# Pinning TensorE to the order of the text in the mixer half of a hybrid encoder layer

## Chip, cores and metric

The kernel runs on one core of one Trainium2 chip. The metric is the device time of one execution in microseconds. TensorE does the matrix products and transposes, VectorE (DVE), ScalarE (ACT) and GpSimd (POOL) the elementwise work, SyncE (SP) issues nearly all transfers. TensorE writes to PSUM, eight banks here, which the other engines read and free.

## The reference, cut to what is computed

One layer on `x` of 1024 positions by 1024 channels in float32:

```python
u = rms_norm(x, g) @ w_in            # 3328 columns, split over three mixers
y_sb = stick_breaking_attention(q, k, v)   # 4 heads of 64, q and k normalised per head
#   z = q.k / 8;  w[t,s] = sigmoid(z[t,s]) * prod_{s<j<t} sigmoid(-z[t,j]),  s < t
y_ret = silu(r_g) * rms_norm(multiscale_retention(rotary(r_q), rotary(r_k), r_v))  # 8 heads
y_conv = silu(layer_norm(depthwise_conv31(glu(c_a, c_gate))))   # 256 channels
x = x + concat(y_sb, y_ret, y_conv) @ w_out
x = x + relu(rms_norm(x) @ w1)**2 @ w2     # 4096 hidden
```

## The kernel before

Products are computed at float32 accuracy from pairs: each operand is split into a high part and a remainder, and `mm3` (L117 to 120) issues three matmuls into one PSUM bank. A weight tile comes in by DMA, is rounded on ScalarE (L181), and its remainder is subtracted on GpSimd or VectorE (L182).

The mixer half, up to some 500 us of the trace, runs in this order. Group 0 of the input projection (the q and k columns of attention's heads 0 and 1, and all of v) goes through all eight banks at once (L199 to 228). Row sums give the reciprocal of each position's norm (`row_stats`, L243), and `row_bcast` (L249 to 256) spreads it over the partitions: VectorE builds a diagonal (L253), TensorE multiplies it with ones (L255), ScalarE copies.

From there the text is a sequence of ticks. `at_tick(t, order, fn)` books a step, `tick(gemm)` (L269) runs the steps booked for this tick in the order of their numbers and then twelve (narrow group: 256 columns wide, later 512) or, in the output projection, nine projection matmuls:

```python
def tick(gemm=None):
    for _, _, fn in sorted(steps.pop(now[0], []), key=lambda x: x[:2]):
        fn()
    if gemm is not None:
        gemm()
    now[0] += 1
```

The order numbers are: 0 a projection tile's evacuation, 5 `sb_turn`, 10 a c-step, 11 to 14 the four steps of a retention tile, 20 a b-step, 25 the convolution's norm, 30 an a-step, 40 taps of the convolution. Ticks 0 to 15 hold the narrow group qk1 (`gemm_narrow`, L424), 16 to 31 the two convolution groups, 32 to 95 four wide groups (k and v of retention's first half, its gate and q, then the same for the second half; `gemm_group`, L444), 96 to 111 the first pass of the output projection (`out_job`, L870), and `while steps: tick()` (L886) what is left.

The steps that ride on these ticks:
- **Attention** (`sb_head`, L340): an a-step multiplies scores into a `z` bank (L353, L355, L356), ScalarE takes two sigmoids (L359, L360), VectorE a running product (L366), GpSimd the weights (L370). Two ticks on, the b-step transposes them into a `t` bank (L381); ScalarE copies (L383) and VectorE subtracts (L384) the pair. The c-step multiplies with v into an `o` bank (L400). 48 a-steps are spread over ticks 6 to 48 by `sb_ticks` (L338), and there are 24 c-steps.
- **`sb_norm` and `sb_turn`**: q and k of a projection tile are normalised (L289 ACT, L292 DVE, L196 POOL, L301 DVE); four tiles are then turned by TensorE (L308, L309) into two `t` banks, which ScalarE (L317, L320, L323) and VectorE (L318, L321, L324) empty. This stands in ticks 3, 6, 9 and 17.
- **Retention** (`ret_chunk`, L649): rotary on VectorE (L563, L565) and GpSimd (L567, L568), then turn, scores, out and back one, two, five and seven ticks later (L660, L671, L682, L715). The gate's evacuation is L729 on ScalarE and L730 on VectorE.
- **Convolution**: 124 taps on VectorE (L592, L595) from tick 35 on, each group held behind the rotary or gate instruction of its tick by `tc.issue_after`.

PSUM has four tags of two banks: `g` for the projection, `t` for what is transposed, `z` for scores, `o` for outputs. After the mixer half comes the second pass of the output projection and the MLP, whose products of two by two blocks use seven multiplications.

The text's order is not the order on an engine. The program is built with

```python
with tile.TileContext(nc, schedule_with_timeline_sim=True) as tc:
```

and the framework orders each engine's instructions by a timeline of its own, in which the place in the text is only a priority: an instruction whose operands are not there yet is passed by later ones. `tc.keep_in_program_order(i)`, which the kernel already uses for some late loads and splits (L107, L807), pins an instruction behind the one traced before it on its engine.

Of the kernel before, what the change touches and what calls it, by code (L numbers as in the profile page):

```python
# [78 lines left out]
def build(tc, d):  # L79
    nc = tc.nc  # L80
# [5 lines left out]
    sm = ctx.enter_context(tc.tile_pool(name="sm", bufs=2))  # L86
    pp = ctx.enter_context(tc.tile_pool(name="pp", bufs=2, space=bass.MemoryType.PSUM))
    dp = ctx.enter_context(tc.tile_pool(name="dp", bufs=1, space=bass.MemoryType.DRAM))
    V, S, GP, TE = nc.vector, nc.scalar, nc.gpsimd, nc.tensor
    uid = [0]  # L90

    def nm(s):
# [172 lines left out]
        steps.setdefault(t, []).append((order, len(steps.get(t, [])), fn))  # L265

    now = [0]

    def tick(gemm=None):  # L269
        for _, _, fn in sorted(steps.pop(now[0], []), key=lambda x: x[:2]):  # L270
# [4 lines that stand above are left out]
# [492 lines left out]
    def split_mixed(k, halves_=(0, 1)):  # L767
        if k not in mh:
            mh[k], ml[k] = slot(where[k][0], dt=F32R), slot(where[k][1], dt=F32R)
        for hf in halves_:  # L770
            cs = slice(512 * hf, 512 * hf + 512)
            src = conv_part(k - 4, hf) if k in (4, 5) else mixed[k][:, cs]
            S.copy(mh[k][:, cs], src)
            V.tensor_tensor(out=ml[k][:, cs], in0=src, in1=mh[k][:, cs].bitcast(F32), op=ALU.subtract)
# [110 lines left out]
            split_mixed(5)  # L885
    while steps:  # L886
        tick()
    for hf in range(2):
        for k in (6, 7):
            split_mixed(k, (hf,))  # L890
# [309 lines left out]
```

## Time and profile before

| | |
|---|---|
| three runs | 1165.1, 1167.29, 1168.1 us; median 1167.29 |
| the profiled execution | 1169.35 us |
| its span on the device | 1167.6 us |
| mean granted TensorE clock | 0.988 of full speed |
| TensorE busy | 1125.4 us (96% of the span) |
| VectorE busy | 899.3 us (77%) |
| ScalarE, GpSimd busy | 483.4 us (41%), 525.8 us (45%) |
| chain that ended last | TensorE 81%, VectorE 10%, waits for DMA 3% |

TensorE is nearly always at work, so the shares of the whole span say little about a single stage. The stretches by time say more: up to 50 us the first group, 50 to 500 the ticks and what follows them, from 500 on the MLP. Busy times of different engines lie side by side. A granted clock of 1.00 is the upper of TensorE's two levels (2.4 GHz), 0.5 the lower one (1.2 GHz).

### The profile page before, as it was taken

What the parts mean: (1) busy time and instruction counts of PE and PEld (TensorE: products, weight loads), DVE (VectorE), ACT (ScalarE), POOL (GpSimd) and SP (SyncE); (2) the same over time, 40 slices, a digit from 0 to 9 for tenths busy, and PEclk for the clock granted to TensorE, in tenths of its full rate; (3) what the DMA queues carried; (4) which work ended last, traced back from release to release, by engine and by line L of the source; (5) the groups of instructions that cost most, each with busy time, mean ns of one, the idle gap of its engine ahead of it and who ended that gap; (6) DMA issues with size and microseconds to landing.
All of it is one profiled execution on the core that took longest, in us unless ns stands there. A gap on an engine that the chain in (4) does not pass through costs nothing.

```text
span 1167.6 us, 15654 instructions
## 1 busy us (share of the span) xinstructions
PE 1125.4 (96%) x5416; PEld 938.2 (80%) x5416; DVE 899.3 (77%) x1378; ACT 483.4 (41%) x917; POOL 525.8 (45%) x413
## 2 busy tenths in 40 slices
PE   8969999999998998899999999999999999999998
PEld 6858788888876887788788888888877788888887
DVE  7487678897998678669975657575699897896964
ACT  7366555543312251255443333333444344444441
POOL 4355334554546363241475565647582542531400
PEclk9989999999999999999999999999999999999999
DMA  7101120120203033022244544353597464453332
GB/s 273 50 1 46 46 60 19 33 87 19 86 19 86 19 140 127 28 90 89 83 160 147 166 148 160 140 171 136 217 333 254 161 201 151 154 183 88 109 127 90
DMA packets 63726, 136.98 MB, mean 117 GB/s; under 512 B 7200, under 2 KB 11936, under 8 KB 63648
## 3 DMA queue, kind: packets, MB, share of 16 engines
q1 hardware_dynamic: 63072, 135.56, 35.0%
q8 instruction: 42, 0.69, 0.2%
q10 hardware_dynamic: 576, 0.44, 0.1%
q14 instruction: 36, 0.29, 0.1%
HBM read 98.22 MB, written 37.75 MB: 116 GB/s over the span
## 4 chain that ended last, share of the span: by engine, by line
PE 81%; DVE 10%; issue 3%; DMA 3%; POOL 2%; ACT 1%; SPq 0%; POOLq 0%; DVEq 0%; ACTq 0%
PE g L118 11%; PE g L119 11%; PE g L120 10%; PE t L120 5%; PE o L119 5%; PE t L118 5%; PE t L119 5%; PE o L118 5%; PE o L120 5%; PE z L118 4%; PE z L119 4%; PE z L120 4%; DVE glu L595 2%; PE o L400 1%; DVE DM__444_2079 L595 1%
## 5 line engine op out<-in xcount | busy, mean ns | idle before, releaser
L182 DVE TENSOR_TENSOR wlo<-sum,whi 128x512 fp32r<-128x512 f32 x78 | 81.7, 1049 | 79.6 <-ACT whi L181 79.5
L181 ACT CAST whi<-sum 128x512 fp32r<-128x512 f32 x78 | 47.9, 617 | 99.2 <-POOL sum L911 47.2
L182 DVE TENSOR_TENSOR wlo<-wr,whi 128x512 fp32r<-128x512 f32 x80 | 76.3, 959 | 6.2 <-ACT whi L181 6.2
L916 POOL TENSOR_TENSOR sum<-wr 128x512 f32<-128x512 f32 x16 | 23.8, 1486 | 115.2 <-DMA wr<-in_w_ff_dram 76.4
L181 ACT CAST whi<-wr 128x512 fp32r<-128x512 f32 x80 | 48.4, 620 | 64.6 <-PE g L119 20.4
L196 POOL TENSOR_TENSOR rs<-ss,nhalf 128x4 f32<-128x4 f32 (+1 forms) x36 | 39.3, 1095 | 77.0 <-DVE ss L703 49.0
L370 POOL TENSOR_TENSOR be<-be,kp 128x512 f32<-128x512 f32 (+3 forms) x48 | 44.4, 927 | 65.1 <-DVE kp L366 26.4
L366 DVE TENSOR_TENSOR_SCAN kp<-kp 128x512 f32<-128x512 f32 (+3 forms) x48 | 52.4, 1098 | 8.0 <-ACT kp L359 7.9
L595 DVE SCALAR_TENSOR_TENSOR glu<-glu,vec 128x512 f32<-128x512 f32 x60 | 52.9, 919 | 0.0
L595 DVE SCALAR_TENSOR_TENSOR DM__444_2079<-glu,vec,DM__444_2079 128x512 f32<-128x512 f32 x60 | 51.6, 897 | 0.1
L911 POOL TENSOR_TENSOR sum<-wr,sum 128x512 f32<-128x512 f32 x19 | 34.0, 1789 | 10.3 <-DVE wlo L182 10.3
L182 POOL TENSOR_TENSOR wlo<-wraw,whi 128x512 fp32r<-128x512 f32 x18 | 28.7, 1603 | 19.8 <-ACT whi L181 19.8
L359 ACT ACTIVATE kp<-z 128x512 f32<-128x512 f32 (+3 forms) x48 | 23.7, 497 | 28.7 <-PE z L356 17.1
L182 POOL TENSOR_TENSOR wlo<-rawq,whi 128x512 fp32r<-128x512 f32 x14 | 23.7, 1690 | 20.8 <-ACT whi L181 20.8
L911 POOL TENSOR_TENSOR sum<-sum,wr 128x512 f32<-128x512 f32 x18 | 25.3, 1404 | 13.8 <-DVE wlo L182 13.8
L567 POOL TENSOR_TENSOR P__543_2611<-P__403_1908 128x128 f32<-128x128 f32 x16 | 15.8, 990 | 26.4 <-DVE P__403_1908 L565 20.5
L360 ACT ACTIVATE be<-z 128x512 f32<-128x512 f32 (+3 forms) x48 | 23.8, 500 | 8.3 <-PE t L381 8.3
L381 PE MATMUL t<-ident,be 128*128 128x128 f32 x144 | 24.8, 275 | 0.2 <-DVE P__494_2387 L384 0.2
L181 ACT CAST whi<-wraw 128x512 fp32r<-128x512 f32 x33 | 20.1, 619 | 11.7 <-PE g L119 3.1
L911 POOL TENSOR_TENSOR wr<-wr,wr 128x512 f32<-128x512 f32 x16 | 23.6, 1477 | 1.1
L671 PE MATMUL z<-P__543_2611,P__544_2612 128*128 128x128 f32 x128 | 18.1, 285 | 3.9 <-DVE P__545_2613 L672 3.9
L181 ACT CAST whi<-rawq 128x512 fp32r<-128x512 f32 x23 | 14.2, 620 | 17.3 <-issue 8.3
(2952 smaller groups left out, 4141.8 us busy)
## 6 DMA issues: line engine op xcount, KB each, us to landing
wr<-in_w_ff_dram SPq DMA_DIRECT2D x40, 512.0 KB, 3.9
wraw<-in_w_in_dram SPq DMA_DIRECT2D x32, 256.0 KB, 2.8
rawq<-in_w_in_dram SPq DMA_DIRECT2D x20, 256.0 KB, 2.8
P__402_1907<-in_rot_dram SPq DMA_DIRECT2D x32, 128.0 KB, 2.1
wraw<-in_w_out_dram SPq DMA_DIRECT2D x10, 256.0 KB, 2.9
rawq<-in_w_out_dram SPq DMA_DIRECT2D x6, 256.0 KB, 2.9
P__18_144<-in_xT_dram SPq DMA_DIRECT2D x1, 512.0 KB, 5.5
P__24_182<-in_xT_dram SPq DMA_DIRECT2D x1, 512.0 KB, 6.5
```

The costliest lines, as they stand in the source:

```text
L118: TE.matmul(out, lh, rh, start=start, stop=False, skip_group_check=on)
L119: TE.matmul(out, lh, rl, start=False, stop=False, skip_group_check=on)
L120: TE.matmul(out, ll, rh, start=False, stop=stop, skip_group_check=on)
L181: S.copy(hi, raw)
L182: (lo_engine or GP).tensor_tensor(out=lo, in0=raw, in1=hi.bitcast(F32), op=ALU.subtract)
L196: GP.tensor_tensor(out=out, in0=in_, in1=nhalf[:, 0:in_.shape[1]], op=ALU.pow)
L360: S.activation(be[:, 0:n], pz[:, 0:n], AF.Sigmoid, scale=0.125)
L366: V.tensor_tensor_scan(rev, rev, rev, kp[:, n:n + 1], op0=ALU.mult, op1=ALU.bypass)
L370: GP.tensor_tensor(out=be[:, 0:n], in0=be[:, 0:n], in1=kp[:, 1:n + 1], op=ALU.mult)
L381: TE.transpose(pt[:, j * P:j * P + P], be[:, j * P:j * P + P], ident)
L595: V.scalar_tensor_tensor(out=acc, in0=src, scalar=vec[:, o:o + 1], in1=acc, op0=ALU.mult, op1=ALU.add)
L911: (eng or GP).tensor_tensor(out=o, in0=x, in1=y, op=ALU.subtract)
```

## The change

A class `TE` takes the place of the engine's handle. Its `matmul` and `transpose` call the engine's, and while `in_order[0]` is set they pin the instruction to its place in the text. The flag is set after the row sums, ahead of `def tick`, and cleared after the last booked step, so it covers every TensorE instruction from the row broadcast through ticks 0 to 111 and the steps after them. No instruction and no transfer is added or taken away; the other engines' instructions are still ordered by the framework.

```diff
--- before.py
+++ after.py
@@ -86,7 +86,24 @@
     sm = ctx.enter_context(tc.tile_pool(name="sm", bufs=2))
     pp = ctx.enter_context(tc.tile_pool(name="pp", bufs=2, space=bass.MemoryType.PSUM))
     dp = ctx.enter_context(tc.tile_pool(name="dp", bufs=1, space=bass.MemoryType.DRAM))
-    V, S, GP, TE = nc.vector, nc.scalar, nc.gpsimd, nc.tensor
+    V, S, GP = nc.vector, nc.scalar, nc.gpsimd
+    in_order = [False]
+
+    class TE:
+
+
+        @staticmethod
+        def matmul(*a, **k):
+            i = nc.tensor.matmul(*a, **k)
+            if in_order[0]:
+                tc.keep_in_program_order(i)
+
+        @staticmethod
+        def transpose(*a, **k):
+            i = nc.tensor.transpose(*a, **k)
+            if in_order[0]:
+                tc.keep_in_program_order(i)
+
     uid = [0]
 
     def nm(s):
@@ -266,6 +283,8 @@
 
     now = [0]
 
+    in_order[0] = True
+
     def tick(gemm=None):
         for _, _, fn in sorted(steps.pop(now[0], []), key=lambda x: x[:2]):
             fn()
@@ -885,6 +904,7 @@
             split_mixed(5)
     while steps:
         tick()
+    in_order[0] = False
     for hf in range(2):
         for k in (6, 7):
             split_mixed(k, (hf,))
```

## Rows read from the trace of the kernel before

**Rows 1.** Busy time by engine over the whole span: us, share, instructions (page, part 1)

```profile
PE 1125.4 (96%) x5416; PEld 938.2 (80%) x5416; DVE 899.3 (77%) x1378; ACT 483.4 (41%) x917; POOL 525.8 (45%) x413
```

**Rows 2.** Windows: stretch, length, busy PE, PEld, DVE, ACT, POOL, granted clock, DMA, GB/s

```profile
60.00:75.00 15.00, 7.95 (x34) 5.87 (x33) 13.54 (x38) 11.19 (x23) 10.19 (x10) 0.67 0.00 0
75.00:121.00 46.00, 41.19 (x282) 37.10 (x281) 35.04 (x72) 26.70 (x57) 21.68 (x21) 1.00 0.10 30
...
165.20:232.20 67.00, 67.00 (x377) 56.90 (x376) 55.22 (x106) 34.48 (x82) 33.74 (x37) 1.00 0.15 44
232.20:301.30 69.10, 68.51 (x399) 59.20 (x398) 59.62 (x110) 28.71 (x69) 34.28 (x32) 1.00 0.20 60
301.30:361.50 60.20, 58.35 (x308) 49.63 (x307) 58.68 (x104) 15.14 (x37) 33.37 (x34) 0.97 0.14 43
361.50:381.50 20.00, 12.84 (x58) 9.48 (x56) 16.07 (x26) 4.66 (x9) 11.33 (x11) 1.00 0.34 96
...
433.00:500.00 67.00, 58.03 (x284) 47.76 (x283) 49.48 (x94) 16.86 (x39) 20.55 (x20) 0.95 0.26 97
500.00:842.00 342.00, 341.28 (x1502) 281.72 (x1503) 241.08 (x313) 140.77 (x232) 185.57 (x127) 1.00 0.41 140
```

**Rows 3.** L381 alone (PE, PEld, clock, DMA); then the timeline's last narrow matmul: start, duration

```profile
50.00:99.40 49.40, 1.61 (x10) 1.13 (x10) 0.90 0.00 1
...
99.11 0.28 PE L120 MATMUL g<-whi,xl__59_380 128*128 128x256 f32 x1
```

**Rows 4.** Timeline of the start: us of start, duration, instruction, idle time before it

```profile
56.45 0.69 DVE L253 TENSOR_TENSOR P__94_487<-ident,rstd 128x512 f32<-128x512 f32 x1
...
68.24 0.47 PE L353 MATMUL z<-P__71_449,P__69_447 128*128 128x128 f32 x1 [3.68 <-DVE P__71_449 L321]
...
72.29 0.48 DVE L366 TENSOR_TENSOR_SCAN kp<-kp 128x128 f32<-128x128 f32 x1
...
72.80 0.74 DVE L366 TENSOR_TENSOR_SCAN kp<-kp 128x256 f32<-128x256 f32 x1
...
73.57 0.43 DVE L301 TENSOR_TENSOR cv<-g,rs 128x256 f32<-128x256 f32 x1
...
74.17 0.46 PE L118 MATMUL g<-whi,xh__12_101 128*128 128x256 f32 x1
```

**Rows 5.** Timeline, 80 to 124 us: a tile's normalisation and the turns' banks

```profile
80.81 0.38 ACT L289 ACTIVATE e<-g 128x256 f32<-128x256 f32 x1 [2.42 <-PE g L120]
...
84.88 0.42 DVE L301 TENSOR_TENSOR cv<-g,rs 128x256 f32<-128x256 f32 x1 [0.64 <-POOL rs L196]
...
87.00 0.27 PE L309 MATMUL t<-ident,cv 128*128 128x128 f32 x1
...
90.88 0.76 DVE L318 SCALAR_TENSOR_TENSOR P__125_577<-t,vec,P__125_577 64x512 fp32r<-64x512 f32 x1
...
118.31 0.66 PE L309 MATMUL t<-ident,cv 128*128 128x128 f32 x4 [0.20 <-DVE P__234_1134 L384]
...
122.65 0.76 DVE L318 SCALAR_TENSOR_TENSOR P__125_577<-t,vec,P__125_577 64x512 fp32r<-64x512 f32 x1
```

**Rows 6.** Timeline, one b-step: its transposes and the subtraction after them

```profile
127.22 0.60 PE L381 MATMUL t<-ident,be 128*128 128x128 f32 x4
...
128.88 0.69 DVE L384 TENSOR_TENSOR P__234_1134<-t,P__233_1133 128x512 fp32r<-128x512 f32 x1 [1.91 <-ACT P__233_1133 L383]
```

**Rows 7.** Window of the convolution's taps alone (L595): DVE busy, count, clock, DMA

```profile
178.00:280.00 102.00, 24.01 (x27) 1.00 0.14 42
```

**Rows 8.** Timeline, a retention tile's gate and the end of its rotary

```profile
389.18 0.47 ACT L729 ACTIVATE e<-g,rstd 128x256 f32<-128x256 f32 x1
...
391.95 0.97 POOL L568 TENSOR_TENSOR P__543_2611<-P__403_1908 128x128 f32<-128x128 f32 x1
```

**Rows 9.** Windows around a drop of the clock (columns as in Rows 2)

```profile
328.00:331.50 3.50, 3.50 (x10) 2.73 (x9) 3.42 (x11) 0.12 (x1) 0.51 (x1) 0.51 0.00 0
331.50:335.00 3.50, 3.50 (x17) 2.89 (x16) 3.50 (x7) 0.48 (x1) 2.86 (x4) 1.00 0.13 37
```

## Prediction

> **What bounds the kernel now.** I read the busy times first: TensorE works 1125.4 of the span's 1167.6 us, so all that any order of its instructions can win is about 42 us, and the region of the change holds only part of that [rows 1]. Then the busy time by stretch [rows 2]. From 500 us on the MLP keeps TensorE at work without a gap (341.28 of 342 us in the stretch shown); it is not touched, and a shift at its start passes straight through to the end. In the region itself TensorE is idle in four places: 7.05 us of 60 to 75, 4.81 of 75 to 121, 1.85 + 7.16 of 301.3 to 381.5, and 8.97 of 433 to 500. In 165 to 301 there is 0.59 us to win. Third, I asked where the attention's transposes (L381) stand beside the text. In the text 21 of them come by tick 15 (tiles of 1, 2, 3, 4, 1, 2, 4, 4 blocks); when the narrow group's last matmul ends, at 99.4 us, 10 have run [rows 3]. So the scheduler does let TensorE pull projection matmuls ahead of attention, whose operands come late over ScalarE, VectorE and GpSimd. The change forbids this, and so does what it says; that it should turn out to be empty I exclude.
>
> **The working, against the profiled 1169.35 us** (span 1167.6, 1.75 around it; 2.06 above the median of 1167.29). The change adds and removes no instruction and no DMA. What it adds is that a TensorE instruction that waits now holds everything behind it. SP's loads and the other queues keep their own order; loads follow buffers that come free, and in the stretches up to 361 us the DMA engines are busy 0 to 0.20 of the time [rows 2], so I cost them at nothing; a load that came late would show as a wait for wlo (L182). The other three engines are scheduled anew around TensorE; that is not to be seen in advance and goes into the bounds.
>
> A, ticks 0 to 5. The row broadcast now stands ahead of tick 0 and waits for VectorE until 57.14 us. That and the turn of tick 3 are covered by what ends this stage anyway: tick 4's matmul at 74.17 waits for a `g` bank that VectorE frees at 74.00 [rows 4], with VectorE busy 13.54 of 15 us [rows 2]. Before, the first scores and the second turn fill this wait, 68.24 to 74.17, 5.9 us at the lower clock [rows 4]. They now come after it, at full clock: +3.0. Their two scans, 0.48 and 0.74 us, no longer stand ahead of the freeing instruction on VectorE [rows 4]: -1.2. Sum **+1.8** (from -1.2, if all the moved work finds later gaps, to +4.0, half of all 7.95 busy us).
>
> B, ticks 6 to 17. A turn (L304) takes both `t` banks, and b-steps, which need one, stand right behind it in ticks 9 and 17. From the transposes to the end of the last L318 on that bank it is 91.64 - 87.27 = 4.4 us, and 123.41 - 118.97 = 4.4 us the second time [rows 5]. Before, projection matmuls run in these times; in text order nothing may: +8.8. The turn of tick 9 also needs tile 3 normalised: its ScalarE square starts at 80.81 for the tile before, VectorE ends 85.30, so 4.5 us [rows 5] against one tick of matmuls, an estimate of 2.4 us (the 41.19 us busy in 75 to 121 [rows 2], over the some 17 ticks whose projection runs there): +2.1. The b-step of tick 8 follows the turn of tick 6 at some 3.5 us of matmuls: 4.4 - 3.5 = +0.9. Together 11.8; the 4.8 us that are idle there now are the same kind of wait and go: **+7.0** (+3 if only one `t` wait is seen in full, +11.8 if the old idle stays).
>
> C, ticks 18 to 61. Nothing to win (0.59 us). A c-step needs its b-step's copy on ScalarE and subtraction on VectorE: from the last transpose's end, 127.82, to 129.57 is 1.75 us [rows 6]. Between them in the text stand twelve matmuls, at 3.50 us for 17 [rows 9] some 2.5 us, so the pair is normally hidden. That cover fails when VectorE has something else in hand. I take one c-step in four of 24, each at one VectorE instruction of 0.69 us [rows 6]: **+4** (0 to 24 x 0.69 = 16.6).
>
> D, ticks 62 to 83. VectorE sets the end here, 58.68 of 60.20 us busy [rows 2]. The convolution's taps (L595) could start earlier only if they ran behind the text now; of the 31 that stand up to tick 57, 27 have run by 280 us [rows 7], and at most two more, the first of a row (L592), which that view leaves out; and each is held behind its own tick's rotary, so there is little to fetch forward. Lateness from A to C passes through: **0** (-9.5, VectorE's idle time of 232 to 301, to +3).
>
> E, ticks 84 to 111. A retention tile's turn waits for ScalarE's L729 and then VectorE and GpSimd: 389.18 to 392.92, 3.7 us [rows 8], against one tick of 2.5 us and its small matmuls, some 0.5. About 0.7 us a tile is left, for six tiles: **+4** (-9.0, if the idle of 433 to 500 closes, to +8).
>
> F, clock. After a wait in TensorE the granted clock was 0.51 over 328.0 to 331.5, its lower level, and 1.00 from there [rows 9]: half of 3.4 us, 1.7, is lost each time. B's longer waits may bring one or two more: **+1.7** (0 to +3.4).
>
> By the Trainium skill, "TensorE: Matmul & The Clock Gate", section "HAM oscillation", a TensorE that idles once in each round of a loop is put back to half rate each round and pays the way back each time. The trace agrees in part only: the drop at 328 is there, but in 75 to 121, with 4.81 us idle in short pieces, the granted clock was 1.00 [rows 2]. By the page B alone would cost four drops rather than one; by the row it costs one.
>
> Sum: 1.8 + 7.0 + 4 + 0 + 4 + 1.7 = 18.5, so 1187.85 for an execution like the profiled one and, 2.06 less, **1185.8** on the median.
>
> **The rivals.**
> - **Faster: the late waits vanish.** Attention comes earlier against the projection, so VectorE finishes its share before tick 62, the taps and retention find it free, and the 18.0 us of idle after 301 (1.85 + 7.16 + 8.97) go [rows 2]. A and B still cost 8.8: 1167.3 - 9.2 = 1158.1. For it: VectorE has 11.8 us idle in 165 to 232 and 9.5 in 232 to 301 [rows 2]. Against: the taps follow their tick, and VectorE's 58.68 of 60.20 leaves no slack to share out. It decides at tick 62: if A to C have cost under 18 us and VectorE's queue is empty there, this one holds.
> - **No change.** A to C are paid back by just those idle times: 12.8 us lost, 9.5 and 3.3 of E's 9.0 won: 1167. It needs two terms to meet by chance.
> - **Much slower: every wait trips the clock.** Each of the 24 c-steps and 16 retention tiles leaves a pause; if four in ten are followed by the lower level, that is 16 x 1.7 = 27 us on top: 1167.3 + 18.5 + 27 = 1213. For it: the drop at 328 [rows 9]; against: none in 75 to 121 [rows 2]. It decides once TensorE's pauses are longer than those. This is also where the rule of the Trainium skill's page named above leads; its own figure, 1.67 us at half rate in each round, would make 40 x 0.83 = 33, an estimate from that page.
>
> **How the numbers follow.** Forecast 0.56, its own range 1172 to 1200 by the bounds. Faster rival 0.23, no change 0.09, much slower 0.12. The range reaches down to 1156, past the middle of the faster rival, and up to 1213, the middle of the slowest; about 0.17 stay outside. A measurement of this kernel can tell about 0.3%, 3.5 us, from no change. Faster 0.23, same 0.09, slower 0.68.
>
> **What would show it.** Right: all 21 transposes of L381 done before tick 16's first matmul; two waits of about 4.4 us of L381 for L318 in ticks 9 and 17; TensorE's idle time in ticks 4 to 17 near 12 us instead of 4.8; L400 waiting now and then for L384; turns of retention (L660) waiting for L568; TensorE's busy time as before, save for half-clock stretches. Wrong, if the two `t` waits are absent (B falls), if TensorE reaches tick 62's matmuls no later than now (A to C fall), if the 7.16 us of 361.5 to 381.5 are gone (the faster rival), or if the granted clock is at its lower level in ten or more stretches (the slowest).

## The result, and the profile after

The changed kernel takes **1200.76 us** (median of 4 runs, 1199.84 to 1202.06) against 1167.69 for the kernel before on the same chips: a ratio of 1.0288, interval 1.0269 to 1.0307, or 33 us more. The profiled execution's span went from 1167.6 to 1198.1 us. In the changed kernel's line numbers every matmul stands at L97 and every transpose at L103, the two calls of the new class; the tile names still tell them apart. Other lines moved down by 17 to 20: the old L318 is L337, L301 is L320, L384 is L403, L710 is L729.

The page's busy times, to be read against [rows 1]:

```profile
PE 1135.2 (95%) x5416; PEld 948.5 (79%) x5416; DVE 888.3 (74%) x1378; ACT 484.3 (40%) x917; POOL 524.4 (44%) x413
```

The same 5416 matmuls take TensorE 9.8 us longer than in [rows 1]; since nothing was added, I put that to the clock, whose lower stretches stand further down. The remaining 20.7 us of the span are idle time. Where it lies is told by the windows of TensorE alone, cut where the changed kernel's stages end (columns: stretch, its length, busy, granted clock, DMA share, GB/s):

```profile
50.00:84.40 34.40, 24.71 (x148) 0.80 0.00 0
84.40:130.00 45.60, 31.59 (x206) 0.84 0.10 30
130.00:334.00 204.00, 198.40 (x1087) 0.99 0.14 44
334.00:415.00 81.00, 69.15 (x320) 0.92 0.17 53
415.00:550.30 135.30, 124.15 (x651) 0.95 0.23 82
```

Length less busy time: idle 9.7 us from 50 us up to tick 8, 14.0 in ticks 8 to 17, 5.6 up to tick 64, 11.9 up to tick 83, 11.2 to the start of the MLP. In [rows 2] the same places held 11.9 (7.05 + 4.81) for the first two, then 0.6, 9.0 and 9.0. So idle time grows by 11.8, 5.0, 2.9 and 2.2, in all 21.9 us; the MLP, idle 5.5 us where it was 6.9, gives 1.3 back.

What the new idle time waits for stands in the waits of TensorE, for 50 to 130, 130 to 350 and 350 to 550 us (total, times, longest):

```profile
PE t L103 <- DVE P__125_577 L337: 6.8, 2, 3.5
PE t L103 <- DVE cv L320: 6.8, 2, 3.6
PE g L97 <- DVE ss L311: 5.2, 1, 5.2
PE o L97 <- DVE P__92_482 L270: 2.8, 1, 2.8
PE t L103 <- DVE P__72_450 L337: 1.7, 1, 1.7
...
PE t L103 <- POOL e L729: 4.5, 1, 4.5
PE o L97 <- DVE P__526_2557 L403: 2.2, 1, 2.2
PE o L97 <- ACT P__525_2556 L402: 1.6, 1, 1.6
...
PE t L103 <- POOL e L729: 10.8, 2, 10.0
PE t L103 <- DVE cv L635: 6.3, 2, 3.1
...
```

The list reads as a list of places in the text. L270 is the diagonal of the row broadcast, L311 stands ahead of tick 4's first matmul, L337 and L320 are the two turns, L402 and L403 one c-step in tick 49, L729 the retention's back step, L635 the second half of the convolution's norm. The place at tick 9 in the timeline (start, duration, instruction, idle time before it):

```profile
85.82 0.99 PE L103 MATMUL t<-ident,cv 128*128 128x128 f32 x6
...
89.50 0.42 DVE L320 TENSOR_TENSOR cv<-g,rs 128x256 f32<-128x256 f32 x1 [1.88 <-POOL rs L213]
89.98 0.44 PE L103 MATMUL t<-ident,cv 128*128 128x128 f32 x2 [3.17 <-DVE cv L320]
...
92.99 0.76 DVE L337 SCALAR_TENSOR_TENSOR P__125_577<-t,vec,P__125_577 64x512 fp32r<-64x512 f32 x1
...
93.89 0.66 PE L103 MATMUL t<-ident,be 128*128 128x128 f32 x2 [3.48 <-DVE P__125_577 L337]
```

Six of the turn's eight transposes run, the last two wait 3.17 us for the tile that has just been normalised, and then the attention's b-step waits 3.48 us for the bank that the turn took. Between the two waits TensorE works 0.4 us. At tick 17 the pair is 3.60 and 3.37.

The clock, in windows of TensorE around each place where it fell:

```profile
54.00:61.00 7.00, 5.49 (x14) 0.51 0.01 2
71.00:78.00 7.00, 6.18 (x29) 0.51 0.00 0
91.50:98.50 7.00, 4.61 (x21) 0.51 0.00 0
122.00:132.50 10.50, 5.95 (x18) 0.52 0.15 50
265.50:269.00 3.50, 3.07 (x13) 0.53 0.56 188
337.00:344.50 7.50, 5.90 (x26) 0.54 0.11 36
378.00:382.00 4.00, 4.00 (x13) 0.57 0.00 0
395.00:399.00 4.00, 4.00 (x12) 0.57 0.00 0
470.50:484.50 14.00, 6.54 (x27) 0.51 0.58 226
```

Nine stretches at the lower level (1.2 GHz) with 45.7 us of work in them, half of which, 22.9, I take as their price. The kernel before has five with 20.4 us of work, so 10.2:

```profile
65.00:75.50 10.50, 6.52 (x27) 0.51 0.00 0
328.00:331.50 3.50, 3.50 (x10) 0.51 0.00 0
382.50:386.00 3.50, 3.50 (x10) 0.52 0.24 67
440.50:444.00 3.50, 3.39 (x16) 0.53 1.02 405
495.00:499.00 4.00, 3.52 (x10) 0.57 0.00 0
```

The difference is 12.7 us by this estimate, 9.8 by the page's busy time. Half is somewhat too much: in the stretch at 378 us a matmul of 512 columns starts 0.43 us after the one before it, and 0.23 us once the clock is back. Each of the nine stands at or just behind a wait of TensorE.

Last, tick 97, with the longest wait. The retention's back step transposes a tile whose chain begins with the square on ScalarE:

```profile
462.23 0.37 ACT L704 ACTIVATE e<-o 128x256 f32<-128x256 f32 x1
462.32 1.28 DVE L793 TENSOR_TENSOR xl__791_4296<-P__121_573,xh__790_4295 128x512 fp32r<-128x512 f32 x2
...
468.73 0.41 DVE L721 TENSOR_REDUCE ss<-e 128x4 f32<-128x256 f32 x1
...
471.63 0.47 DVE L722 TENSOR_SCALAR ss<-ss 128x4 f32<-128x4 f32 x1
...
473.61 2.72 DVE L614 SCALAR_TENSOR_TENSOR glu<-glu,vec 128x512 f32<-128x512 f32 x4
476.25 0.41 DVE L726 TENSOR_TENSOR e<-o,rs 128x256 f32<-128x256 f32 x1
476.75 1.16 POOL L729 TENSOR_TENSOR e<-e,P__715_3749 128x256 f32<-128x256 f32 x1 [2.79 <-DVE e L726]
477.96 0.69 PE L103 MATMUL t<-ident,e 128*128 128x128 f32 x2 [10.03 <-POOL e L729]
```

The square is done at 462.60, but VectorE takes up its sum only at 468.73: splits of the output projection's operands (L793) stand ahead of it. Later the convolution's taps (L614) stand ahead of L726. VectorE is busy 13.98 of the 14.06 us from 462.60 to 476.66; the short instructions that TensorE waits for stand behind long ones that it does not wait for here.

### The profile page after: what moved, and what is told of

Read it like the earlier page. It is cut to its first block, busy times and chain, and to the rows that moved or that the text cites. A ratio compares the mean times of both kernels' runs of the same rounds, so it can differ in the third digit from the quotient of the medians.

```text
span 1198.1 us, 15632 instructions
## 1 busy us (share of the span) xinstructions
PE 1135.2 (95%) x5416; PEld 948.5 (79%) x5416; DVE 888.3 (74%) x1378; ACT 484.3 (40%) x917; POOL 524.4 (44%) x413
## 4 chain that ended last, share of the span: by engine, by line
PE 85%; DVE 7%; issue 2%; POOL 2%; DMA 2%; ACT 1%; SPq 0%; ACTq 0%; POOLq 0%; DVEq 0%
PE g L97 34%; PE o L97 18%; PE z L97 16%; PE t L97 15%; PE t L103 3%; DVE DM__444_2079 L614 1%; DVE glu L614 1%; DVE kp L385 1%; DVE wlo L199 0%; DMA P__402_1907<-in_rot_dram 0%; DMA wraw<-in_w_in_dram 0%; POOL wlo L199 0%; POOL rs L213 0%; POOL be L389 0%; DVE P__403_1908 L584 0%
## 5 line engine op out<-in xcount | busy, mean ns | idle before, releaser
L389 POOL TENSOR_TENSOR be<-be,kp 128x512 f32<-128x512 f32 (+3 forms) x48 | 46.9, 981 | 87.0 <-DVE kp L385 73.8
L614 DVE SCALAR_TENSOR_TENSOR DM__444_2079<-glu,vec,DM__444_2079 128x512 f32<-128x512 f32 x60 | 49.3, 864 | 0.0
L614 DVE SCALAR_TENSOR_TENSOR glu<-glu,vec 128x512 f32<-128x512 f32 x60 | 46.8, 820 | 0.0
L103 PE MATMUL t<-ident,be 128*128 128x128 f32 x144 | 24.4, 286 | 9.0 <-DVE P__125_577 L337 6.8
L103 PEld LDWEIGHTS t<-ident,be 128*128 128x128 f32 x144 | 17.3, 145 | 11.7 <-issue 9.3
L582 DVE SCALAR_TENSOR_TENSOR P__403_1908<-g,rstd,P__402_1907 128x256 f32<-128x256 f32 x32 | 15.3, 478 | 10.7 <-PE g L97 10.7
```

Of the source, the lines that this page charges most:

```text
L103: i = nc.tensor.transpose(*a, **k)
L389: GP.tensor_tensor(out=be[:, 0:n], in0=be[:, 0:n], in1=kp[:, 1:n + 1], op=ALU.mult)
L614: V.scalar_tensor_tensor(out=acc, in0=src, scalar=vec[:, o:o + 1], in1=acc, op0=ALU.mult, op1=ALU.add)
```

## The experiments

All run on the chip against the kernel before; ratios are to its runs on the same chip; gains are told against the changed kernel's 1200.8, losses against the kernel before beside each run, whose median lies between 1166.6 and 1168.9 on these chips. Diffs are against the changed kernel.

**Which ticks cost.** Two runs cut the pinned stretch at tick 18:

```diff
-    in_order[0] = True
     def tick(gemm=None):
+        if now[0] == 18:
+            in_order[0] = True
```

> Pinned only from tick 18 on; the row broadcast and ticks 0 to 17 are ordered by the framework as before. Theory (the loss sits in a few places of the text, each with its own price): the two turns behind whose transposes b-steps wait cost about 17 us with their half-clock stretches, the start 3 us; without them about 1181 us, and the waits of 4.5 and 10.0 us of the transposes at L103 for L729 stay. Rival (VectorE's work sets when the later stages end, so a gain ahead of tick 18 is lost again behind it): about 1197 to 1201 us, with longer waits after tick 60.

Measured: 1192.88 us (ratio 1.021, 1.0181 to 1.0238), between the two. Only 8 us came back. The rival is not the reason: the waits for L729 and L635 are the changed kernel's, 15.3 and 6.3 us in all. The first turn's waits and the start's went, but not all of the second turn's, since the first pinned instruction still stands behind everything traced ahead of it, the turn of tick 17 among it. In its waits one for the bank is left, and ahead of it one of 2.2 us for L403:

```profile
PE t L103 <- DVE P__125_577 L337: 3.2, 1, 3.2
```

The other half, pinned from the start and freed at tick 18:

```diff
     in_order[0] = True
     def tick(gemm=None):
+        if now[0] == 18:
+            in_order[0] = False
```

> Pinned only up to tick 17; from tick 18 on ordered by the framework. Theory (local places): the loss of the start and the two turns, some 20 us, stays: about 1187 us. Rival (what is lost early is made good by idle time of TensorE later, 9 us in ticks 62 to 83 and 9 us in the output projection's first pass): about 1170 to 1176 us.

Measured: 1177.11 us (1.0072, 1.0048 to 1.0096), +9.5, again between. Up to 124 us TensorE is idle 20.3 us here, and it works 22.4 us at the lower clock level in the stretches that begin there (the last runs to 129), against 11.9 and 6.5 before: +8.4 idle and, by the estimate above, +8.0 for the clock, 16.4. Of that only 9.5 arrive at the end, 8.0 in the spans of the profiled executions. Part is made good: its windows (TensorE, columns as above) show 17.1 us idle behind 124 where the kernel before has 18.6, and two low-clock stretches fewer, with 6.9 us of work where there were 13.9: 5 us together. That leaves 11.4; the other 2 us or more these windows don't place. The second turn's wait for its banks is absent here: 24 projection matmuls, from 123.44 to 131.66 us, run between that turn and tick 17's b-step, since those of the ticks behind it are not pinned.

```profile
50.00:124.00 74.00, 53.66 (x342) 0.85 0.05 16
124.00:300.00 176.00, 175.53 (x966) 0.99 0.15 44
300.00:510.00 210.00, 193.38 (x1025) 0.98 0.22 71
```

Two more runs pin the rest in two pieces. The middle, where TensorE had no idle time:

```diff
-    in_order[0] = True
     def tick(gemm=None):
+        if now[0] in (21, 62):
+            in_order[0] = now[0] == 21
```

> Pinned in ticks 21 to 61 alone, where TensorE has no idle time in the kernel before. Theory (the pinned order costs only its own waits, here for L402 and L403 near tick 49, 3.8 us and a low-clock stretch): 1168 to 1175 us. Rival (attention that keeps up with the projection leaves VectorE free later, so the idle time after tick 62 closes): 1152 to 1161 us.

Measured: 1180.87 us (1.0095, 1.0075 to 1.0116), +12.0: worse than the theory said, and on the other side from the rival. Attention that keeps up with the projection does not close the idle time behind tick 62: 14.5 us of it stay of 18.0, among them one wait of 6.6 us for a back step. The price is paid in the pinned middle, idle 8.7 us between 121 and 310 us where the kernel before had 0.6 (3.8 of it the wait for L403 in tick 49), and in the clock, 38.1 us of work at the lower level against 20.4.

```profile
PE t L103 <- POOL e L729: 7.3, 2, 6.6
```

And the end:

```diff
-    in_order[0] = True
     def tick(gemm=None):
+        if now[0] == 62:
+            in_order[0] = True
```

> Pinned from tick 62 on alone. Theory (the waits of 4.5, 3.15, 3.15 and 10.0 us and their low-clock stretches, less the idle time that is there before): 1177 to 1185 us. Rival (these waits come from lateness that the pinned ticks 0 to 61 hand on): 1165 to 1172 us.

Measured: 1174.94 us (1.0057, 1.0038 to 1.0075), +6.1, just under the theory's bound. The waits are those of the changed kernel, though nothing ahead of tick 62 is pinned:

```profile
PE t L103 <- POOL e L729: 13.7, 5, 10.0
PE t L103 <- DVE cv L635: 6.3, 2, 3.1
```

So they don't come from lateness handed on; they are made by the text of these ticks. They cost little net, because the idle time that the kernel before has there goes at the same time. The three pieces together, 9.5 + 12.0 + 6.1 = 27.6, leave 5.5 of the 33.1 us. Ticks 18 to 20, which none of the three pins, stand for it with the second turn's wait for its banks, and so does whatever the pieces do to each other; no run separates these.

**The turns' banks.** The turn takes one bank from each of two tags:

```diff
-        pq, pk = bank("t"), bank("t")
+        pq, pk = bank("t"), bank("o")
```

> Pinned as in the change, but a turn takes one t bank and one o bank, so that a b-step behind it finds a t bank free. Theory (b-steps wait for the turn's banks): the waits of 3.5 and 3.4 us for L337 go, with half-clock time behind them some 9 us: about 1191 us. Rival (the turn's late operands are the cause, and the b-step's own operands are no earlier): the wait moves to the b-step's operands or to the c-step, 1198 to 1201 us.

Measured: 1192.16 us (1.0204, 1.0177 to 1.023), -8.6, as the theory had it. The two waits for L337 behind the turns are gone from the list; those for the normalisation stay and grow by a little:

```profile
PE t L103 <- DVE cv L320: 8.1, 2, 4.5
```

**The turns' place.** Here the operands get a tick more:

```diff
-            at_tick(now[0] + 1, 5, lambda: sb_turn(1, tt // 4))
+            at_tick(now[0] + 2, -1, lambda: sb_turn(1, tt // 4))
```

> Pinned as in the change, but the two turns of the narrow group stand a tick later, ahead of that tick's other steps (ticks 10 and 18 instead of 9 and 17), so that the last of their four tiles has a tick more to be normalised; they still take both t banks. Theory (two causes, one after the other in each place): the waits of 3.2 and 3.6 us for L320 shrink to under 1 us each, those for L337 stay: about 1194 us. Rival (one cause: VectorE is that late whatever stands there): waits for L337 grow by as much, 1199 to 1202 us.

Measured: 1195.32 us (1.0247, 1.0231 to 1.0262), -5.4. Nearer to the theory: the normalisation's waits fall from 6.8 to 2.0, those for the banks rise from 6.8 to 8.0.

```profile
PE t L103 <- DVE cv L320: 2.0, 1, 2.0
```

**The retention's back step.**

```diff
-        at_tick(t + 7, 11, back)
+        at_tick(t + 9, 11, back)
```

> Pinned as in the change, but the last step of a retention tile (back, L729 to L737) stands nine ticks behind the tile instead of seven. Theory (it is only too close behind its producers in the text): the waits of 4.5 and 10.0 us for L729 shrink to 0 to 5 us and two low-clock stretches go: about 1186 to 1190 us. Rival (VectorE is simply behind there, and whatever comes next waits for it): the wait moves to L671, L682 or L660 and the time stays within 1197 to 1202 us.

Measured: 1185.04 us (1.0142, 1.0111 to 1.0173), -15.7, a little more than the theory gave. No wait for L729 is left. In their place, at 464.7 us, stands one of 3.0 us for the next tile's rotary, and the convolution's longest wait grows from 3.1 to 4.2 us:

```profile
PE t L103 <- POOL P__543_2611 L587: 4.1, 2, 3.0
```

**The convolution's norm.**

```diff
-        at_tick(t + 2, 25, lambda t2=t2: conv_norm_b(t2))
+        at_tick(t + (4 if t2 > 1 else 2), 25, lambda t2=t2: conv_norm_b(t2))
```

> Pinned as in the change, but the second half of the convolution's norm for its first two pairs of tiles stands four ticks behind the first half instead of two (ticks 76 and 80). Theory (two waits of 3.15 us for L635 and the low-clock stretches of 4 us of work behind each): 6.3 + 4 us less, about 1191 us. Rival (VectorE sets the end of that stage, so its waits move to the next place, the retention's first steps or the wait of 10 us at tick 97): 1198 to 1201 us.

Measured: 1198.5 us (1.0272, 1.0255 to 1.0289), -2.3, which the two intervals don't tell from nothing. The rival holds: the two waits for L635 leave but for 0.2 us, and the retention's first transposes of the second half wait 3.6 us for L587 instead, with smaller waits around them. In this stage VectorE sets the end, as [rows 2] showed before, and moving one step only moves the wait.

```profile
PE t L103 <- POOL P__543_2611 L587: 3.6, 1, 3.6
```

**Together.** Bank and back step first:

> Pinned, with the turn's second bank from o and the retention's back step at nine ticks, both together. Theory (each place has its own price, and prices add up): 1200.8 less 8.6 less 15.8, about 1176 us. Rival (what is won ahead of tick 18 is lost again in VectorE's stages): about 1184 us, as with the later back step alone.

Measured: 1177.41 us (1.0095, 1.008 to 1.011), 1.0 from the sum of the two single gains, or 2.0 when each is taken against the kernel before on its own chip. Within the noise, these two prices, at places far apart, add up. With all four edits:

> Pinned, with all four edits: turn's second bank from o, turn a tick later, back step at nine ticks, convolution's norm at four. Theory (the loss sits in these places): 1200.8 less 8.6, 15.8, some 9 and some 6: about 1161 to 1168 us, level with the kernel before or better. Rival (VectorE's work is the bound behind the waits): not under 1175 us.

Measured: 1174.65 us (1.0071, 1.0053 to 1.0089): the theory missed, by 6.7 us and more, and the rival's bound of 1175 is nearly met. The two weaker edits bring 2.8 us where they brought 5.4 and 2.3 alone. TensorE's idle time is down to 34.2 us, near the 30.4 of the kernel before, but it comes in pieces that bring the lower clock level: 32.9 us of work at it against 20.4.

**Without pinning.** The same four edits, and no flag set:

> The four edits of the run before last (turn's bank from o, turn a tick later, back at nine ticks, convolution's norm at four) without any pinning: the kernel before with these edits alone. Theory (the edits mend what pinning breaks; where TensorE may pass a waiting instruction they bring nothing): 1164 to 1171 us. Rival (the edits are a gain of their own, so the pinned kernel with them still hides a loss of its own): 1150 to 1160 us.

Measured: 1154.0 us (0.987, 0.9855 to 0.9884): the rival. The edits are more than a repair of the pinning: of the 26.1 us that they win in the pinned kernel, 14.9 come without pinning too. With the edits in the text the pinning still costs 1174.65 - 1154.0 = 20.6 us (22.9 against the kernel before on each chip) instead of 33.1. Which of the edits gains without pinning, tried with the back step at nine ticks alone:

> The kernel before, without any pinning, with the retention's back step at nine ticks as its only edit. Theory (the gain of the four free edits is the back step's, as it was the largest of the four in the pinned kernel): 1152 to 1158 us, and TensorE's idle time of 364 to 381 and 435 to 450 us shrinks. Rival (the gain belongs to the turns or the convolution's norm, or to all together): 1163 to 1169 us.

Measured: 1155.03 us (0.9872, 0.9843 to 0.99), so it is the back step, nearly alone. Its windows, from the slowest of its four executions, against the two in [rows 2] that held most of the late idle time:

```profile
361.50:381.50 20.00, 15.23 (x58) 10.65 (x58) 15.43 (x22) 4.92 (x9) 12.21 (x12) 0.91 0.35 109
433.00:500.00 67.00, 63.59 (x314) 52.26 (x313) 50.07 (x98) 20.82 (x40) 21.93 (x22) 1.00 0.30 106
```

Up to the MLP the idle time falls from 30.4 to 20.9 us. That of 433 to 500 goes from 8.97 to 3.41 us, that of 361.5 to 381.5 from 7.16 to 4.77. These two versions beat both kernels; they can't be told from each other.

## Why the prediction was right, and where it was too small

Direction and mechanism held: TensorE waits at places where the text puts a step close behind its producers, and the framework's order used to fill them. The time, 1200.8, lies in the range and just past the forecast's own, 1172 to 1200. The forecast itself was little more than half of the loss, 18.5 us against 30.5 in the spans. By term:

- **A and B** (ticks 0 to 17), 8.8: idle time grew by 11.8, of which 0.7 came up to tick 8 and 11.1 behind it, where B had 7.0. The 5.9 us that A halved, 68.24 to 74.17, hold 5.2 us of work, and A expected this work to run at full clock once moved; instead 11.7 us of work of this stage ran at the lower level, against 6.5 before (54 to 61 and 71 to 78 above). All 21 transposes of L381 had run before tick 16's first matmul, at 116.0 us, as the text asks (tile `be` alone, to 113.3):

```profile
50.00:113.30 63.30, 3.97 (x21) 0.84 0.00 1
```

  The bank waits were there, at 3.5 and 3.4 us rather than 4.4. What was left out is the turn of tick 17: B charged a wait for the last tile's normalisation at tick 9 alone, 2.1 us, and it was 3.2 there and 3.6 at tick 17. The rows for it were the same; the step was only looked at once.
- **C**, 4: +5.0. Not one c-step in four by 0.7 us, though: most of it is one c-step, in tick 49. Its copy (L402, at 262.71) stood behind a rounding on ScalarE that waited for a weight load, and its subtraction (L403, at 265.20) behind two taps of 2.64 us together and L171 on VectorE. The size was right by luck.

```profile
262.18 0.62 ACT L170 CAST ww<-wraw 128x512 fp32r<-128x512 f32 x1 [1.84 <-DMA wraw<-in_w_in_dram]
```

- **D**, 0, and **E**, 4: +2.9 and +2.2. The sums were near by luck, the working was not. D held that lateness passes through; instead the back step and the convolution's norm made waits of their own, and the old idle time went. E named the turn behind L568, which waited 0.9 us; the back step behind L710 (L729 after) waited 10.0. It stands two ticks behind its out-step, as every b-step stands behind its a-step, but its chain crosses VectorE three times, and each time it can fall behind other work.
- **F**, 1.7: this is the term that failed. The busy time grew by 9.8 us. "One or two more" low-clock stretches was taken from [rows 9] and the quiet stretch of 75 to 121; there were four more, and several two to four times as long as the one in [rows 9]. The longest three stand behind the pair at tick 17, the wait of 10.0 us and the one of 4.5 us; what sets their length no run here shows. The Trainium skill, "TensorE: Matmul & The Clock Gate", section "HAM oscillation", has the lower rate come back with each round of a loop that idles. Here it came back at each place with 2.8 us or more of waiting, nine times, while single waits of 0.7 to 1.7 us were not followed by it. The length of a wait alone does not decide it: in the kernel before, the drop of [rows 9] stands behind a wait of 1.84 us, and the clock stayed at 1.00 [rows 2] behind one of 2.17.

```profile
327.02 0.44 PE L715 MATMUL t<-ident,e 128*128 128x128 f32 x2 [1.84 <-POOL e L710]
...
366.65 0.50 PE L119 MATMUL g<-wlo,xh__40_265 128*128 128x512 f32 x1 [2.17 <-DVE wlo L182]
```

The rival of the many drops was half right: nine stretches, one short of its ten, and 12.7 us by the work at the lower level (22.9 less 10.2), where it said 27.

The **faster rival** fell twice. Idle time behind 301 us did not close in the changed kernel, 23.0 us against 18.0, and with the middle pinned alone the kernel got 12 us slower. "**No change**" by paying back was partly seen: of 16.4 us lost up to tick 17, 9.5 reached the end.

That SP's loads cost nothing held for TensorE itself, none of whose listed waits is for a load; but one reached it through ScalarE, at tick 49. It was not the whole price there: with the middle pinned alone, ScalarE's copy was done by 251.4 us and TensorE still waited 3.8 us for VectorE, up to 255.6. What remains open: each edit also gives the other engines a new order, and no run separates that from the order of TensorE. Open too is whether VectorE would take the retention's chain first if its order were set by hand. That was not tried; the later back step only goes around it.

## What to carry to other kernels

When an engine is made to keep the text's order, go through the text for every step that stands close behind its producers, every time it occurs, and price the chain by what may stand ahead of each link on the other engines, not by its bare length. Then add the clock: of a loss of TensorE here a third was work at the lower level behind the waits. And where a pinned order shows one long wait, try giving that step more distance in the order that the framework makes too. Here the step was already waited for in the kernel before, the 1.84 us above, and this one number was worth 13 us, while none of the pinnings tried gained anything.

## What was not expected of the hardware

Taken as half of the work, as above, the price of a stretch at the lower level goes by the work that falls into it, not by how long it lasts. Over 470.5 to 484.5 us the granted clock was 0.51 for 14 us, from within the 10.0 us wait on, and this held only 6.5 us of work, so it cost 3.3. Over 378 to 382 it was at the lower level for 3.4 of 4.0 us, full of work, and cost 1.7 behind a wait of 3.15. Two short waits were thus dearer in clock, for each us that they idled, than the one long wait.
